# A mixture-of-experts stage whose experts are ranked by row count: big ones as before, small ones in 64-row tiles

## The chip, the cores and the metric

The kernel runs on one core of a Trainium2 chip. The metric is the device time of one execution in microseconds (us); the median of several executions is compared.

## The reference, cut to what matters

A decoder block: two mixers (causal pooling and sparse attention), a residual, and then a mixture of 32 gated-MLP experts with top-2 routing inside one of four groups. Everything is float32. The change touches the experts alone:

```python
for each expert e, with the rows xb of h2 that were routed to it:   # 1024 tokens, 2 experts each
    a  = silu(xb @ w_gate[e]) * (xb @ w_up[e])    # (n_e, 2048) @ (2048, 512), twice
    ys = a @ w_down[e]                            # (n_e, 512) @ (512, 2048)
    out[token] += ys * gate                       # 2048 rows in all, 64 an expert on average
x = x + gt2 * out
return rmsnorm(x, g_final)
```

Each expert's weights are 12 MiB and are read once, 384 MiB in all.

## The kernel before

The routing runs on the chip. `tables` leaves `sidx` (128 x 32, int32: for each expert and slot the token, or a number past the end for an empty slot), `sgat` (the gates, same layout) and `cnt` (rows of each expert, on every partition).

Then the experts run one after the other, 0 to 31. An expert has `CAP` = 112 slots. `gather` fetches its token rows from the scratch tensor `h2_d` by an indirect DMA from GpSimd's queue (L1221); slots past the end move nothing. `columns_of` transposes the 128 x 2048 rows on TensorE in sixteen 128 x 128 pieces (L1232) and splits each group of four into a high part `xh`, rounded to the matmul's fast fp32 type by ScalarE, and a rest `xl`, by VectorE (both L112, in `split`).

Weights come in twelve 1 MiB chunks an expert (`weight_chunks`: four of gate, four of up, four of down), issued by SyncE (`load`, L1246) into thirteen `raw` buffers, about one expert ahead; the buffer order is the order of use. `halves` splits a chunk in two steps into `hi` (ScalarE) and `lo` (VectorE), each 128 x 1024. `mm3` then forms one product as three fast matmuls, hi x hi, lo x hi, hi x lo (L117, L120, L121; 128 x 512 columns each). An expert has 32 such products for gate and up and 16 for down, 144 matmuls.

In `hidden` the next expert's columns are transposed between the up and the down matmuls (`nxt`), so that TensorE has work while sigmoid and the products of `sg` are formed (L1269 to L1271). `expert` ends with the gating of the output: ScalarE multiplies by the gate (L1295), GpSimd by the row `gt2` (L1296). `scatter` adds the rows to `ya_d` by an indirect DMA (L1300). The last expert isn't scattered: a tail adds its rows by a matmul with a one-hot `pick`, adds `ya_d` and normalises the eight token blocks (L1498 to L1527).

Between the first nine weight loads and the first expert stands a loop for overflow (`For_i`): its trip count, read by every engine from `ni`, is the number of extra blocks of rows of experts with more than 112 rows; it is computed by VectorE from `cnt` (L1371 to L1383). A trip would compute one expert with buffers of its own.

The order of instructions on each engine is that of the program, moved by the framework's scheduler except where `last(...)` pins it.

Elsewhere in the kernel unsplit fp32 matmuls already run: L418 multiplies 32-column stationaries by 512 columns of `w_ada`, the outputs cycling over four strips of 32 partitions; L916 uses one strip alone; L1009 forms the router's logits.

Of the kernel before, what the change touches and what calls it, by code (L numbers as in the profile page):

```python
# [19 lines left out]
P = 128  # L20
D = 2048
KT = D // P
S = 1024
# [4 lines left out]
TINY = 1.1754944e-38  # L28
RATE, RATE2 = 27, 19
NH = 8  # L30
CAP = 112
NE = 32
NG = 4
DE = 512
# [40 lines left out]
def hybrid_block(ctx, tc, x, c, w_ada, b_ada, g_mix, w_in, w_pool, pool_scale, rel_bias, w_out,  # L75
# [32 lines left out]
    def tr_ps():  # L108
        return psum.tile([P, 512], F32, name="tr", bufs=4)
# [841 lines left out]
    rk = rt.tile([P, 2, NB], F32, name="rk")  # L951
    cnt = rt.tile([P, NE], F32, name="cnt")
    sidx = rt.tile([P, NE], I32, name="sidx")
    sgat = rt.tile([P, NE], F32, name="sgat")
    gt2r, gfr = [rt.tile([KT, P], F32, name=n) for n in ("gt2r", "gfr")]
    with ExitStack() as es:
# [108 lines left out]
        def tables(hf):  # L1065
# [30 lines left out]
            nc.vector.tensor_add(tb0, tb0, pa[:, :96])  # L1096
            nc.vector.tensor_scalar(dmp, tb0[:, 64:], -1.0, 1.0, op0=OP.mult, op1=OP.add)
            nc.vector.tensor_scalar(dmp, dmp, pid, float(S), op0=OP.mult, op1=OP.add)
            nc.vector.tensor_add(sidx, dmp, tb0[:, :32])
            nc.vector.tensor_copy(sgat, tb0[:, 32:64])  # L1100
            pc = tr_ps()
            for i in range(NB):
# [111 lines left out]
                finish(1, st)  # L1214
    wo1.close()

    def gather(A, idx, fill=False):
        xg = A.xg()
        if fill:
            nc.gpsimd.memset(xg, 0.0)  # L1220
        nc.gpsimd.indirect_dma_start(out=xg[:CAP], out_offset=None, in_=h2_d,  # L1221
                                     in_offset=bass.IndirectOffsetOnAxis(ap=idx[:CAP], axis=0),
                                     bounds_check=S - 1, oob_is_err=False)
        return xg

    def columns_of(A, xg):
        xh, xl = A.xh(), A.xl()
        for k4 in range(4):
            pt = tr_ps()
            for j in range(4):  # L1230
                k = k4 * 4 + j
                nc.tensor.transpose(pt[:, j * P:(j + 1) * P], xg[:, k * P:(k + 1) * P], ident)  # L1232
            ks = slice(k4 * 4, k4 * 4 + 4)
            split(xh[:, ks, :], xl[:, ks, :], pt.rearrange("p (a b) -> p a b", b=P))
        return xh, xl
# [22 lines left out]
    def hidden(A, chunks, xh, xl, nxt=None):  # L1258
        pgu = []
        for _ in range(2):  # L1260
            ps, k = mm_ps(), 0
            for k0 in range(0, KT, 4):
                for w in halves(A, chunks()):
                    mm3(ps, (xh[:, k, :], xl[:, k, :]), w, k == 0, k == KT - 1)
                    k += 1
            pgu.append(ps)
        wd0 = halves(A, chunks())
        sg = A.sg()
        nc.scalar.activation(sg, pgu[0], AF.Sigmoid)  # L1269
# [14 lines left out]
    def expert(A, chunks, gt2, xh, xl, gate, nxt=None):  # L1284
        ah, al, w, res = hidden(A, chunks, xh, xl, nxt)
# [12 lines left out]

    def scatter(y, idx):
        nc.gpsimd.indirect_dma_start(out=ya_d, out_offset=bass.IndirectOffsetOnAxis(ap=idx[:CAP], axis=0),  # L1300
                                     in_=y[:CAP], in_offset=None, compute_op=OP.add,
                                     bounds_check=S - 1, oob_is_err=False)

    class Tiles:
# [7 lines left out]
        def sg(self):  # L1312
            return self.x.tile([P, DE], F32, name="sg")

        def ah(self):
            return self.x.tile([P, 4, P], F32R, name="ah")

        def al(self):
            return self.m.tile([P, 4, P], F32R, name="al")

        def xh(self):
            return self.m.tile([P, KT, P], F32R, name="xh")

        def xl(self):
            return self.m.tile([P, KT, P], F32R, name="xl")
# [34 lines left out]
    srcs = [c_ for e in range(NE) for c_ in weight_chunks(w_gate[e], w_up[e], w_down[e])]  # L1360
    early = deque(load(A, srcs.pop(0)) for _ in range(9))
    xgs = deque(gather(A, sidx[:, e:e + 1], True) for e in range(2))


    NOV = 20
    with ExitStack() as es:
        ov = pool_of(es, "ov")
        slot = ov.tile([P, P], F32, name="slot")
        nc.gpsimd.iota(slot, pattern=[[1, P]], base=0, channel_multiplier=0, allow_small_or_imprecise_dtypes=True)
        nb = ov.tile([P, NE], F32, name="nb")  # L1370
        nc.vector.tensor_scalar(nb, cnt, float(CAP), None, op0=OP.is_gt)  # L1371
        for j in range(2, -(-S // CAP)):
            nc.vector.scalar_tensor_tensor(nb, cnt, float(j * CAP), nb, op0=OP.is_gt, op1=OP.add)
        ce = nb
        d = 1
        while d < NE:
# [12 lines left out]
        ei = ov.tile([P, NE], F32, name="ei")  # L1389
        nc.gpsimd.iota(ei, pattern=[[1, NE]], base=0, channel_multiplier=0, allow_small_or_imprecise_dtypes=True)  # L1390
        nc.gpsimd.iota(od, pattern=[[1, NOV]], base=0, channel_multiplier=0, allow_small_or_imprecise_dtypes=True)
        nov = nc.values_load(ni[0:1, 0:1], min_val=0, max_val=NOV - 1)
        with tc.For_i(0, nov, 1) as it:
            with ExitStack() as e2:
# [9 lines left out]
                nc.vector.tensor_scalar(oj, oj, 1.0, float(CAP), op0=OP.add, op1=OP.mult)  # L1404
                nc.vector.tensor_scalar(oi, oe_, float(NE - 1), None, op0=OP.min)
                ej = lp.tile([P, 2], F32, name="ej")
                nc.vector.tensor_copy(ej[:, 0:1], oe_[:, bass.ds(it, 1)])
                nc.vector.tensor_copy(ej[:, 1:2], oj[:, bass.ds(it, 1)])
                ex_ = nc.values_load(oi[0:1, bass.ds(it, 1)], engines=[mybir.EngineType.SP], min_val=0,
                                     max_val=NE - 1)  # L1410
                oh1 = lp.tile([P, NE], F32, name="oh1")
                nc.vector.tensor_scalar(oh1, ei, ej[:, 0:1], None, op0=OP.is_equal)
                pt_ = tr_ps()
                for t in range(NB):
                    for j in range(2):
# [21 lines left out]
                xh, xl = columns_of(B, gather(B, ix, True))  # L1437
                parts = iter(list(weight_chunks(*[w[bass.ds(ex_, 1)].rearrange("o a b -> (o a) b")
                                                  for w in (w_gate, w_up, w_down)])))
                y, _ = expert(B, lambda: load(B, next(parts)), g2_, xh, xl, od_[:, 1:2])  # L1440
                scatter(y, ix)

    m = pool_of(mo_, "mo")
    A.m, A.halves = m, [(mh, 2), (mh, 2), (m, 2), (m, 2)]
    A.raws += [(m, 4)] * 4
    early.extend(load(A, srcs.pop(0)) for _ in range(4))
    xe = columns_of(A, xgs.popleft())

    def chunks():
        return early.popleft() if early else load(A, srcs.pop(0))  # L1450

    for e in range(NE - 1):
        def nxt(e=e):
            x_ = columns_of(A, xgs.popleft())
            if e + 2 < NE:
                xgs.append(gather(A, sidx[:, e + 2:e + 3]))
            return x_

        y, xe = expert(A, chunks, gt2, *xe, sgat[:, e:e + 1], nxt)
        scatter(y, sidx[:, e:e + 1])  # L1460


    ah, al, w, _ = hidden(A, chunks, *xe)
# [3 lines left out]
    nc.vector.tensor_copy(sid, sidx[:, NE - 1:NE])  # L1467
# [19 lines left out]
    for n4 in range(4):  # L1487
        if n4 % 2 == 0:
            yh, yl = A.hilo()
        gated(y, py[n4], sgat[:, NE - 1:NE], gt2, n4)  # L1490
        ys.append((yh[:, n4 % 2, :], yl[:, n4 % 2, :]))
        split(*ys[n4], y[:, n4 * 512:(n4 + 1) * 512])

# [74 lines left out]
```

## Time and profile before

| | us |
|---|---|
| median of 3 executions | 2880.85 (2875.68 to 2884.74) |
| profiled execution: its own time | 2879.47 |
| profiled execution: span, first to last instruction | 2877.6 |
| mean granted TensorE clock over the span | 0.96 of 2.4 GHz |

The rows further down are of that one profiled execution; their times count from the first instruction. Busy time of an engine is the time in which at least one of its instructions ran. A matmul's record lasts longer than the step from one matmul to the next, since matmuls overlap; the step is read from the starts.

### The profile page before, as it was taken

The numbers are of one execution on the slowest core, as the hardware profiler recorded it, in microseconds if no ns is written. First come the engines' busy times: TensorE is split into PE (matmuls) and PEld (weight loads), VectorE is DVE, ScalarE is ACT, GpSimd is POOL, SyncE is SP. The second block draws the span as 40 slices with busy tenths as digits, with TensorE's granted clock in tenths as the row PEclk, the third lists the DMA queues.
The fourth block names the chain that finished last, engine by engine and source line by source line (L and its number), as shares of the span: only waits on it lengthen the run. The fifth ranks groups of instructions, "written<-read, shape, count | busy, mean of one in ns | idle before, by whom it ended". The sixth has DMA issues, their size and how long they took to land.

```text
span 2877.6 us, 37030 instructions
## 1 busy us (share of the span) xinstructions
PE 2571.0 (89%) x11968; PEld 2041.0 (71%) x11968; DVE 2172.6 (75%) x3098; ACT 1851.6 (64%) x2856; POOL 1129.9 (39%) x943
## 2 busy tenths in 40 slices
PE   6978888999988899999985999999999999999994
PEld 3667677887756677788874777777777777777773
DVE  6798776888853773344437888888888888888988
ACT  6636777888544773243234777777777777777775
POOL 2286877655863310434222333233332233332222
PEclk8989999999999999999997999999999999999996
DMA  8734555666566614544466999999999999999974
GB/s 306 266 121 125 160 157 149 203 208 191 168 197 208 173 38 162 179 156 144 161 227 236 346 349 350 345 344 341 340 346 346 360 352 348 342 356 341 347 263 166
DMA packets 301223, 713.47 MB, mean 248 GB/s; under 512 B 33196, under 2 KB 189956, under 8 KB 243236
## 3 DMA queue, kind: packets, MB, share of 16 engines
q1 hardware_dynamic: 292960, 678.04, 66.4%
q0 software_dynamic: 8064, 33.02, 5.0%
q8 instruction: 96, 1.57, 0.2%
q14 instruction: 103, 0.84, 0.1%
HBM read 655.37 MB, written 80.38 MB: 256 GB/s over the span
## 4 chain that ended last, share of the span: by engine, by line
PE 52%; DVE 16%; ACT 9%; issue 9%; DMA 8%; POOL 4%; SPq 1%; ACTq 0%; DVEq 0%; POOLq 0%
PE mm L117 14%; PE mm L120 14%; PE mm L121 13%; DMA adw<-in_w_ada_dram 5%; DVE lo L112 3%; POOL adacc L526 3%; PE tr L1232 2%; ACT y L1295 2%; ACT adp L521 2%; ACT hi L112 2%; PE tr L120 1%; PE tr L117 1%; PE tr L121 1%; DVE wlo L112 1%; ACT tk_junk L560 1%
## 5 line engine op out<-in xcount | busy, mean ns | idle before, releaser
L112 DVE TENSOR_TENSOR lo<-raw,hi 128x1024 fp32r<-128x1024 f32 x768 | 972.0, 1318 | 130.6 <-ACT hi L112 126.0
L112 ACT CAST hi<-raw 128x1024 fp32r<-128x1024 f32 x768 | 778.7, 1053 | 217.0 <-PE mm L121 210.1
L526 POOL TENSOR_TENSOR adacc<-adacc,adp 128x256 f32<-128x256 f32 x480 | 428.7, 894 | 194.7 <-ACT adp L521 169.2
L120 PE MATMUL mm<-lo,xh 128*128 128x512 f32 x1024 | 412.3, 403 | 43.0 <-DVE lo L112 42.8
L121 PE MATMUL mm<-hi,xl 128*128 128x512 f32 x1024 | 400.1, 391 | 0.0
L117 PE MATMUL mm<-hi,xh 128*128 128x512 f32 x1024 | 398.8, 391 | 0.0
L1296 POOL TENSOR_TENSOR y<-y,gt 128x512 f32<-128x512 f32 x124 | 258.1, 2112 | 189.8 <-ACT y L1295 189.8
L521 ACT ACTIVATE adp<-adw,cs 128x256 f32<-128x256 f32 x480 | 235.9, 505 | 149.8 <-DMA adw<-in_w_ada_dram 73.5
L1221 POOL DMA_INDIRECT xg<-h_d,sidx x32 | 48.9, 1529 | 667.7 <-PE tr L1232 639.1
L120 PEld LDWEIGHTS mm<-lo,xh 128*128 128x128 f32 x1024 | 192.3, 188 | 127.9 <-DVE lo L112 91.5
L117 PEld LDWEIGHTS mm<-hi,xh 128*128 128x128 f32 x1024 | 192.5, 188 | 41.0
L121 PEld LDWEIGHTS mm<-hi,xl 128*128 128x128 f32 x1024 | 192.5, 188 | 36.8 <-DVE xl L112 0.7
L120 PE MATMUL mm<-hTl,whi 128*128 128x512 f32 (+1 forms) x544 | 206.4, 380 | 9.9 <-DVE hTl L476 8.7
L117 PE MATMUL mm<-hTh,whi 128*128 128x512 f32 (+1 forms) x544 | 206.3, 381 | 0.9 <-ACT whi L112 0.9
L121 PE MATMUL mm<-hTh,wlo 128*128 128x512 f32 (+1 forms) x544 | 204.3, 377 | 1.3 <-DVE wlo L112 1.3
L120 PE MATMUL mm<-lo,ah 128*128 128x512 f32 x512 | 201.3, 393 | 0.0
L112 DVE TENSOR_TENSOR olo<-oraw,ohi 128x1024 fp32r<-128x1024 f32 x64 | 93.0, 1455 | 135.9 <-ACT ohi L112 135.8
L121 PE MATMUL mm<-hi,al 128*128 128x512 f32 x512 | 187.9, 398 | 0.0
L688 DVE SCALAR_TENSOR_TENSOR sc<-ev,wi,sc 128x512 f32<-128x512 f32 (+3 forms) x150 | 135.1, 937 | 58.5 <-ACT ev L684 58.3
L121 PE MATMUL mm<-ohi,ml 128*128 128x512 f32 x448 | 175.7, 392 | 0.0
L117 PE MATMUL mm<-ohi,mh 128*128 128x512 f32 x448 | 175.6, 393 | 0.0
L120 PE MATMUL mm<-olo,mh 128*128 128x512 f32 x448 | 175.4, 392 | 0.0
(370 smaller groups left out, 5416.8 us busy)
## 6 DMA issues: line engine op xcount, KB each, us to landing
raw<-in_w_gate_dram SPq DMA_DIRECT2D x128, 1024.0 KB
raw<-in_w_up_dram SPq DMA_DIRECT2D x128, 1024.0 KB
raw<-in_w_down_dram SPq DMA_DIRECT2D x128, 1024.0 KB
adw<-in_w_ada_dram SPq DMA_DIRECT2D x512, 128.0 KB
wt<-in_w_ada_dram SPq DMA_DIRECT2D x64, 512.0 KB
oraw<-in_w_out_dram SPq DMA_DIRECT2D x64, 512.0 KB
wraw<-in_w_in_dram SPq DMA_DIRECT2D x60, 512.0 KB
xt<-in_x_dram SPq DMA_DIRECT2D x8, 1024.0 KB
```

The source lines that it names most:

```text
L112: for i in (nc.scalar.copy(hi, src), nc.vector.tensor_sub(lo, src, hi.bitcast(F32))):
L117: i = nc.tensor.matmul(o, a[0], b[0], start=first, stop=False)
L120: nc.tensor.matmul(o, a[0], b[1], start=False, stop=False)
L121: nc.tensor.matmul(o, a[1], b[0], start=False, stop=final)
L521: last(nc.scalar.mul(dst, adw.pop(i), cs[:, k:k + 1]))
L526: nc.gpsimd.tensor_add(acc[r, n], acc[r, n], adp.pop(i))
L560: nc.scalar.activation(jk, sc[b], AF.Sign, bias=t, scale=1.0, accum_out=cn[:, j:j + 1])
L688: nc.vector.scalar_tensor_tensor(sc[b][:, c0:c0 + w], rl[:, :w], wi[:, b, h:h + 1], sc[b][:, c0:c0 + w], op0=OP.mult, op1=OP.add)
L1221: nc.gpsimd.indirect_dma_start(out=xg[:CAP], out_offset=None, in_=h2_d, in_offset=bass.IndirectOffsetOnAxis(ap=idx[:CAP], axis=0), bounds_ ...
L1232: nc.tensor.transpose(pt[:, j * P:(j + 1) * P], xg[:, k * P:(k + 1) * P], ident)
L1295: nc.scalar.mul(y[:, ns], py[n4], gate)
L1296: nc.gpsimd.tensor_mul(y[:, ns], y[:, ns], gt2[:, ns])
```

## The change

The ranking: a key per expert (32 x rows + 31 - index; expert 0 gets the greatest) is compared with all others, which gives each expert a place. A one-hot matrix `moved` of places permutes the slot tables by matmul into `pidx`, `pgat` and the list `ordi` of expert numbers in order of place. Places 0 to 15 are big (112 slots, computed as before), 16 to 31 small (`CAP2` = 64 slots). They run in the order 0, 16, 17, 1, 18, 2, 19, ..., 14, 31, 15: two small ones at first, then alternating, with a big one last. Expert 0 is always first, and its weights are addressed statically; the others' by a number that SyncE reads from `ordi`.

A small expert transposes 64 rows only and keeps the columns unsplit (`xT`). Its weight chunks are not split either: plain fp32 matmuls read the raw chunk, with 64-column stationaries; even and odd contraction steps go to the two halves of the partitions of one bank, and `folds` (two identities on top of each other) adds the halves and transposes them in one matmul. The down product puts two of its four column ranges in each half. The gating is one VectorE operation for each 512 columns, in big experts too.

The overflow loop counts blocks past 112 or 64 slots.

```diff
-CAP = 112
+CAP, CAP2, NBIG = 112, 64, 16
...
-            nc.vector.tensor_add(sidx, dmp, tb0[:, :32])
+            nc.vector.tensor_add(sidf, dmp, tb0[:, :32])
+            nc.vector.tensor_copy(sidx, sidf)
...
+    def few_columns_in_steps(A, xg, pin=None):
+        xT = A.xT()
+        for k8 in range(2):
+            pt = tr_ps()
+            for j in range(8):
+                k = k8 * 8 + j
+                i = nc.tensor.transpose(pt[:, j * CAP2:(j + 1) * CAP2], xg[:CAP2, k * P:(k + 1) * P],
+                                        ident[:CAP2, :CAP2])
+                if pin and k == 0:
+                    pin(i)
+            nc.scalar.copy(xT[:, k8 * 8:k8 * 8 + 8, :], pt.rearrange("p (a b) -> p a b", b=CAP2))
+            yield xT
...
         for n4 in range(4):
-            ns = slice(n4 * 512, (n4 + 1) * 512)
-            nc.scalar.mul(y[:, ns], py[n4], gate)
-            nc.gpsimd.tensor_mul(y[:, ns], y[:, ns], gt2[:, ns])
+            gated(y, py[n4], gate, gt2, n4)
         return y, res
...
+    def few(A, chunks, gt2, xT, gate, nxt):
+        pf = tr_ps()
+        sums = [A.sg(), A.us()]
+        sig, aT = A.sig(), A.aT()
+
+        def fold(i):
+            for f in range(4):
+                nc.tensor.matmul(pf[:, (i * 4 + f) * CAP2:(i * 4 + f + 1) * CAP2], sums[i][:, f * P:(f + 1) * P], folds,
+                                 start=True, stop=True)
+
+        for i in range(2):
+            ps, k = mm_ps(), 0
+            for k0 in range(0, KT, 4):
+                raw = chunks()
+                for j in range(4):
+                    h = k % 2 * CAP2
+                    nc.tensor.matmul(ps[h:h + CAP2, :], xT[:, k, :], raw[:, j, :], start=(k < 2), stop=(k >= KT - 2))
+                    k += 1
+                if i == 1 and k0 == 4:
+                    fold(0)
+                    nc.scalar.activation(sig, pf[:, :4 * CAP2], AF.Sigmoid)
+                    nc.vector.tensor_mul(sig, sig, pf[:, :4 * CAP2])
+            nc.scalar.copy(sums[i][:, :256], ps[:, :256])
+            nc.vector.tensor_copy(sums[i][:, 256:], ps[:, 256:])
+        steps = nxt()
+        for _, res in zip(range(3), steps):
+            pass
+        fold(1)
+        nc.vector.tensor_mul(aT.rearrange("p a b -> p (a b)"), sig, pf[:, 4 * CAP2:])
+        for res in steps:
+            pass
+        py = [mm_ps() for _ in range(2)]
+        for k in range(4):
+            raw = chunks()
+            for n4 in range(4):
+                h = n4 % 2 * CAP2
+                nc.tensor.matmul(py[n4 // 2][h:h + CAP2, :], aT[:, k, :], raw[:, n4, :], start=(k == 0), stop=(k == 3))
+        y = A.y()
+        for n4 in range(4):
+            h, ns = slice(n4 % 2 * CAP2, n4 % 2 * CAP2 + CAP2), slice(n4 * 512, (n4 + 1) * 512)
+            nc.vector.scalar_tensor_tensor(y[:CAP2, ns], py[n4 // 2][h, :], gate[h], gt2[h, ns], op0=OP.mult, op1=OP.mult)
+        return y, res
...
+        e = nc.values_load(ordi[0:1, r:r + 1], engines=[mybir.EngineType.SP], min_val=0, max_val=NE - 1)
+        return weight_chunks(*[w[bass.ds(e, 1)].rearrange("o a b -> (o a) b") for w in (w_gate, w_up, w_down)])
...
-    xgs = deque(gather(A, sidx[:, e:e + 1], True) for e in range(2))
+    x0 = gather(A, sidx[:, 0:1], fill=True)
...
+        nc.vector.scalar_tensor_tensor(key, cnt, float(NE), kb, op0=OP.mult, op1=OP.add)
+        nc.vector.scalar_tensor_tensor(own, key[:NE], 1.0, ident[:NE, :NE], op0=OP.mult, op1=OP.mult,
+                                       accum_out=place[:, 0:1])
+        nc.vector.tensor_scalar(own, key[:NE], place[:, 0:1], 0.0, op0=OP.is_gt, op1=OP.add, accum_out=place[:, 1:2])
+        nc.vector.tensor_scalar(place[:, 2:3], place[:, 1:2], float(NBIG), None, op0=OP.is_ge)
+        nc.vector.tensor_scalar(flag, ident[:NE, :NE], place[:, 2:3], None, op0=OP.mult)
+        pk = tr_ps()
+        last(nc.tensor.matmul(pk[:, :NE], onesb[:NE, :], flag, start=True, stop=True))
+        nc.vector.tensor_scalar(cap, pk[:, :NE], float(CAP2 - CAP), float(CAP), op0=OP.mult, op1=OP.add)
+        nc.vector.tensor_scalar(moved, ei[:NE], place[:, 1:2], None, op0=OP.is_equal)
+        nc.vector.tensor_sub(over, cnt, cap)
...
-    early.extend(load(A, srcs.pop(0)) for _ in range(4))
-    xe = columns_of(A, xgs.popleft())
+    early.extend(load(A, next(srcs)) for _ in range(3))
+    cols = columns_of(A, x0)
...
+    for i, t in enumerate((sidf, sgat)):
+        nc.tensor.transpose(pt[:NE, i * P:(i + 1) * P], t, ident)
+    nc.scalar.copy(flip, pt[:NE, :2 * P].rearrange("e (a p) -> e a p", p=P))
+    pm = tr_ps()
+    for i in range(2):
+        nc.tensor.matmul(pm[:, i * NE:(i + 1) * NE], flip[:, i, :], moved, start=True, stop=True)
+    nc.tensor.matmul(pm[:NE, 2 * NE:3 * NE], pid[:NE, 0:1].to_broadcast([NE, NE]), moved, start=True, stop=True)
+    nc.vector.tensor_copy(ordi, pm[0:1, 2 * NE:3 * NE])
...
+    for i in range(NE - 1):
+        def nxt(i=i):
+            yield from (columns_in_steps if seq[i + 1] < NBIG else few_columns_in_steps)(A, xgs.popleft(), last)
+            if i + 2 < NE:
+                xgs.append(gather_of(i + 2))
+
+        big, r = seq[i] < NBIG, seq[i]
+        y, cols = (expert if big else few)(A, chunks, gt2, cols, pgat[:, r:r + 1], nxt)
+        scatter(y, pidx[:, r:r + 1], CAP if big else CAP2)
```

`columns_in_steps` is `columns_of` as a generator that yields after each of its four groups. `gather` and `scatter` take the number of slots.

## Rows read from the trace of the kernel before

**Rows 1.** The page: GB/s in 40 equal slices; indirect queue (packets, MB, share).

```profile
GB/s 306 266 121 125 160 157 149 203 208 191 168 197 208 173 38 162 179 156 144 161 227 236 346 349 350 345 344 341 340 346 346 360 352 348 342 356 341 347 263 166
...
q0 software_dynamic: 8064, 33.02, 5.0%
```

**Rows 2.** Windows: length, busy us (instructions) of each engine, clock, DMA share, GB/s.

```profile
core 0: us, PE busy (x) PEld busy (x) DVE busy (x) ACT busy (x) POOL busy (x), PEclk, DMA share, GB/s
2200.00:2300.00 100.00, 92.89 (x423) 73.11 (x423) 88.03 (x83) 74.23 (x86) 25.77 (x13) 1.00 0.98 356
44.00:46.00 2.00, 1.73 (x10) 0.57 (x13) 0.34 (x2) 0.00 (x0) 0.00 (x0) 0.50 0.75 237
1540.00:1549.00 9.00, 0.00 (x0) 0.00 (x0) 0.15 (x1) 0.24 (x1) 0.17 (x2) 0.50 0.32 96
1600.00:2700.00 1100.00, 1019.82 (x4582) 800.55 (x4583) 969.67 (x868) 822.69 (x950) 334.85 (x167) 1.00 0.96 348
1730.00:1740.00 10.00, 8.51 (x43) 6.68 (x42) 9.32 (x12) 7.39 (x10) 0.00 (x0) 1.00 1.01 419
2000.00:2010.00 10.00, 10.00 (x45) 8.01 (x44) 9.43 (x10) 8.39 (x9) 0.00 (x0) 1.00 0.99 331
2776.00:2786.00 10.00, 8.58 (x35) 6.12 (x34) 8.38 (x6) 7.93 (x9) 9.72 (x5) 1.00 0.00 2
2804.00:2810.00 6.00, 6.00 (x28) 4.96 (x27) 5.57 (x6) 4.29 (x5) 0.00 (x0) 1.00 1.02 426
```

**Rows 3.** Waits from 1600 to 2700 us: total us, times, longest us.

```profile
SPq L1246 <- DVE lo L112: 962.0, 335, 6.0
...
ACT hi L112 <- PE mm L121: 181.2, 258, 1.5
...
PEld mm L120 <- DVE lo L112: 82.2, 105, 1.0
...
ACT hi L112 <- DMA raw<-in_w_gate_dram: 2.4, 2, 1.2
```

**Rows 4.** Groups, 1700 to 2700 us: count, busy us, mean ns, idle before, releasers.

```profile
L112 DVE TENSOR_TENSOR lo<-raw,hi 128x1024 fp32r<-128x1024 f32 x610 | 772.7, 1321 | 103.6 <-ACT hi L112 100.9
L112 ACT CAST hi<-raw 128x1024 fp32r<-128x1024 f32 x610 | 617.6, 1053 | 168.1 <-PE mm L121 162.9 <-DMA raw<-in_w_gate_dram 2.4 <-DVE lo L112 0.6
...
L1232 PE MATMUL tr<-ident,xg 128*128 128x128 f32 x408 | 64.7, 276 | 0.3
```

**Rows 5.** Timeline of PE: split matmuls, fp32 in strips, logits.

```profile
2028.01 0.39 PE L117 MATMUL mm<-hi,xh 128*128 128x512 f32 x1
...
2029.82 0.39 PE L121 MATMUL mm<-hi,xl 128*128 128x512 f32 x1
...
44.52 6.66 PE L418 MATMUL tr<-wt,csz 128*32 128x512 f32 x28
...
1499.13 1.08 PE L1009 MATMUL tr<-wr,h2T 128*128 128x36 f32 x8 [0.73 <-ACT h2T L1004]
```

**Rows 6.** Timeline of the end: last weight loads, last casts, gating.

```profile
2757.33 13.63 SPq L1246 DMA_DIRECT2D raw<-in_w_down_dram  x4
...
2807.34 2.01 ACT L112 CAST hi<-raw 128x1024 fp32r<-128x1024 f32 x2 [0.27 <-PE mm L121]
...
2812.39 2.73 DVE L1282 SCALAR_TENSOR_TENSOR y<-mm,sgat,gt 128x512 f32<-128x512 f32 x4 [1.61 <-issue]
```

**Rows 7.** Groups over the whole span: the fp32 matmul in one strip.

```profile
L916 PE MATMUL tr<-ra,ones 128*32 128x512 f32 x32 | 17.4, 626 | 2.4 <-DMA ra<-acc_d 2.4
```

**Rows 8.** Timeline from the row counts to the first expert.

```profile
1536.39 1.77 DVE L1373 SCALAR_TENSOR_TENSOR nb<-cnt,nb 128x32 f32<-128x32 f32 x8
...
1540.04 0.15 DVE L1383 CAST ni<-ce 128x1 int32<-128x1 f32 x1
...
1549.14 1.97 SPq L1246 DMA_DIRECT2D raw<-in_w_down_dram  x3
...
1550.10 3.68 PE L1232 MATMUL tr<-ident,xg 128*128 128x128 f32 x16 [10.48 <-DVE sid L1467]
```

More of the change, by code (lines that the diff above doesn't have):

```diff
@@ L953, in hybrid_block @@
     sidx = rt.tile([P, NE], I32, name="sidx")
+    sidf = rt.tile([P, NE], F32, name="sidf")
     sgat = rt.tile([P, NE], F32, name="sgat")
@@ L1215, in hybrid_block, with gather @@
     wo1.close()
-    def gather(A, idx, fill=False):
+    def gather(A, idx, rows=CAP, fill=False):
         xg = A.xg()
@@ L1220, in gather, with columns_in_steps @@
             nc.gpsimd.memset(xg, 0.0)
[L1221 to L1222 removed]
+        nc.gpsimd.indirect_dma_start(out=xg[:rows], out_offset=None, in_=h2_d,
+                                     in_offset=bass.IndirectOffsetOnAxis(ap=idx[:rows], axis=0),
                                      bounds_check=S - 1, oob_is_err=False)
         return xg
[L1226 removed]
+    def columns_in_steps(A, xg, pin=None):
         xh, xl = A.xh(), A.xl()
@@ L1302, in scatter @@
+    def scatter(y, idx, rows=CAP):
+        nc.gpsimd.indirect_dma_start(out=ya_d, out_offset=bass.IndirectOffsetOnAxis(ap=idx[:rows], axis=0),
+                                     in_=y[:rows], in_offset=None, compute_op=OP.add,
                                      bounds_check=S - 1, oob_is_err=False)
@@ L1359, in hybrid_block, with weights_of @@
     spread(gt2, gt2r)
-    srcs = [c_ for e in range(NE) for c_ in weight_chunks(w_gate[e], w_up[e], w_down[e])]
-    early = deque(load(A, srcs.pop(0)) for _ in range(9))
-    xgs = deque(gather(A, sidx[:, e:e + 1], True) for e in range(2))
-    NOV = 20
+    def weights_of(r):
+        if r == 0:
+            return weight_chunks(w_gate[0], w_up[0], w_down[0])
+        e = nc.values_load(ordi[0:1, r:r + 1], engines=[mybir.EngineType.SP], min_val=0, max_val=NE - 1)
+        return weight_chunks(*[w[bass.ds(e, 1)].rearrange("o a b -> (o a) b") for w in (w_gate, w_up, w_down)])
+    seq = [0, NBIG, NBIG + 1]
+    for r in range(1, NBIG - 1):
+        seq += [r, r + NBIG + 1]
+    seq.append(NBIG - 1)
+    assert sorted(seq) == list(range(NE))
+    srcs = (c_ for r in seq for c_ in weights_of(r))
+    early = deque(load(A, next(srcs)) for _ in range(9))
+    x0 = gather(A, sidx[:, 0:1], fill=True)
+    ordi = mg.tile([1, NE], I32, name="ordi")
+    pidx = mg.tile([P, NE], I32, name="pidx")
+    pgat = mg.tile([P, NE], F32, name="pgat")
+    folds = mg.tile([P, CAP2], F32, name="folds")
+    moved = mg.tile([NE, NE], F32, name="moved")
+    nc.gpsimd.tensor_add(folds, ident[:, :CAP2], ident[:, CAP2:])
+    NOV = 24
     with ExitStack() as es:
@@ L1436, in hybrid_block @@
                 row_bc(g2_, row_d[3])
-                xh, xl = columns_of(B, gather(B, ix, True))
+                cols = columns_of(B, gather(B, ix, fill=True))
                 parts = iter(list(weight_chunks(*[w[bass.ds(ex_, 1)].rearrange("o a b -> (o a) b")
                                                   for w in (w_gate, w_up, w_down)])))
-                y, _ = expert(B, lambda: load(B, next(parts)), g2_, xh, xl, od_[:, 1:2])
+                y, _ = expert(B, lambda: load(B, next(parts)), g2_, cols, od_[:, 1:2])
                 scatter(y, ix)
@@ L1445, in hybrid_block, with gather_of @@
     A.raws += [(m, 4)] * 4
-    early.extend(load(A, srcs.pop(0)) for _ in range(4))
-    xe = columns_of(A, xgs.popleft())
-    def chunks():
[L1450 to L1463, printed above, removed]
+    early.extend(load(A, next(srcs)) for _ in range(3))
+    cols = columns_of(A, x0)
+    flip = A.us()[:NE, :2 * P].rearrange("e (a p) -> e a p", p=P)
+    pt = tr_ps()
+    for i, t in enumerate((sidf, sgat)):
[6 more added lines that the diff above has]
+    nc.vector.tensor_copy(ordi, pm[0:1, 2 * NE:3 * NE])
+    nc.vector.tensor_copy(pidx, pm[:, :NE])
+    nc.vector.tensor_copy(pgat, pm[:, NE:2 * NE])
+    nc.vector.tensor_copy(pgat[CAP2:, NBIG:], pm[:CAP2, NE + NBIG:2 * NE])
+    def chunks():
+        return early.popleft() if early else load(A, next(srcs))
+    def gather_of(i):
+        return gather(A, pidx[:, seq[i]:seq[i] + 1], CAP if seq[i] < NBIG else CAP2, i == 1)
+    xgs = deque([gather_of(1)])
+    for i in range(NE - 1):
[6 more added lines that the diff above has]
+        scatter(y, pidx[:, r:r + 1], CAP if big else CAP2)
+    r_last = seq[-1]
+    ah, al, w, _ = hidden(A, chunks, *cols)
     ids, pick = A.xg()[:, :S], A.xg().bitcast(F32R)[:, :S]
```

56 lines of the change are left out of this document (38 added, 18 removed).

## The prediction

> **What bounds the kernel now.** I read the slices of the page first: from about 1580 us to 2730 us, the experts, the traffic stands at 340 to 360 GB/s where it is 38 to 306 before [rows 1]. So the stage comes close to some limit of the transfers, and the question is whether they set its pace. The windows say that they don't quite: over 1600 to 2700 us DMA is 0.96 busy at 348 GB/s, PE is busy 93%, its granted clock is 1.00 [rows 2]. The waits decide. SyncE, which issues the weight loads, spent 962 of 1100 us waiting for VectorE's lo, that is, for a weight buffer to come free, and the one engine that reads arriving weights, ScalarE's cast, waited for a load only 2.4 us in all [rows 3]. So loads arrive early and are held back by the consumer. The consumer is a ring of three engines: the cast waits for PE, lo for the cast, PE for lo [rows 3, 4]. One expert takes 39.2 us: 408 token transposes at 16 an expert are 25.5 experts in 1000 us [rows 4]. Of these PE is busy 0.93 x 39.2 = 36.3 us: 144 matmuls at 0.226 us (eight steps from 2028.01 to 2029.82 us [rows 5]) are 32.6, the 16 transposes 64.7 / 25.5 = 2.5 [rows 4], the rest is small. VectorE's lo take 24 x 1.32 = 31.7 and the casts 24 x 1.05 = 25.3 us an expert.
>
> How early the loads are shows at the end: the last four weight loads are issued from 2757 us on, DMA moves only 2 GB/s from 2776 us, and the last weight chunk is cast from 2807.3 us [rows 2, 6]. So about 31 us of lead, most of an expert.
>
> **The change, part by part.**
>
> *Small experts on PE.* A small expert drops 144 matmuls, 24 casts, 24 lo, and gains 48 unsplit fp32 matmuls of 512 columns whose outputs alternate between the two halves of the partitions. The nearest row is L418: 28 records, 14 fp32 matmuls over four column tiles, take 6.66 us at a clock of 0.50, that is 1.2 GHz [rows 2, 5]: 0.476 us each. (An fp32 matmul leaves two records: L916 runs 16 times and leaves 32 [rows 7].) Half as many tiles cost twice that, the full clock (2.4 GHz) halves it again: 0.476 us, and 48 are 22.8 us. If tiles didn't overlap at all, one would cost 4 x 0.476 / 2 = 0.95 us, and 48 would be 45.7 us. L916, one tile alone, agrees with this end: busy 17.4 us for 16, 1.09 us each [rows 7]. I take 22.8, because L418 alternates tiles as the new code does. To it come eight folds at the price of the logits matmuls, 8 records in 1.08 us, 0.27 each [rows 5], 2.2 us; the transposes of the next expert, 2.5 us; and two short waits around the folds, which other transposes partly cover, say 1.5 us: 29 us. Bounds: 27 with no waits, 52 with no overlap.
>
> The Trainium skill (TensorEngine Tiling (Array Packing), Key Properties) says that tiles run in parallel, but that a change of tiling mode drains the engine; against the change, then, there are some six changes of mode in a small expert. A matmul's latency beyond its issue step is 0.39 - 0.226 = 0.16 us [rows 5], so an estimate by that rule is 1 us an expert, inside the bounds above.
>
> *The big experts* keep their matmuls. The gating moves from ScalarE and GpSimd to four VectorE operations, 2.73 us together in the last expert of before [rows 6]; the next expert is mostly a small one without lo, so nothing urgent stands behind them, and its transposes need no split, which saves four VectorE operations. I keep 39.2 us; bounds 36.3 (PE alone) and 42 (the gating uncovered).
>
> *The pair.* Compute: 39.2 + 29 = 68 us where it was 78.4. So the ring stops being the limit, and the weights, whose bytes don't change, become it.
>
> *What DMA needs for an expert.* Twelve loads of 1 MiB are 12.58 MB; gathers and scatters moved 33.02 MB in 63 transfers [rows 1], two of them 1.05 MB. Those bytes don't change: 33.02 MB is 4028 rows of 8 KB, the real rows, not the 112 slots. Fastest: weights alone ran at 419 and 426 GB/s [rows 2], 30.0 us, and the indirect queue took 5.0% of 16 engines' span [rows 1]: 0.05 x 2877.6 x 2 / 63 = 4.6 us; 34.6 together. Slowest: the share as it stands, 0.96 x 39.2 = 37.6, or 38.3 by the fullest 100 us, 0.98 busy at 356 GB/s [rows 2]. Near which? At 2000 to 2010 us the engines are 0.99 busy and move only 331 GB/s [rows 2]: indirect packets also slow the weights beside them, which speaks for the upper end; shares of 1.01 and 1.02 [rows 2] count some packets twice, which speaks for a little less. I take 37.2 us (366 GB/s); with 13 buffers and a consumer 6 us a pair faster DMA has always something to load.
>
> *The start.* The ranking adds about ten VectorE operations of 0.2 us (eight of that size took 1.77 us [rows 8]) and a matmul ahead of the count that the overflow loop reads. Every engine stands still from that count (1540.0 us) until 1549.1 us, although the loop runs no trip [rows 2, 8], so nothing hides it: +2.5 us, all engines resume at 1551.6. The first expert's transposes take 3.7 us [rows 8]; the table of ranks follows on PE (two transposes, three matmuls), with a ScalarE copy and four VectorE copies, some 3.5 us; then SyncE reads the second expert's number and can load it: first bytes at about 1562 us (1558 if the table is built ahead of the transposes, 1568 if the register read is as slow as the loop's). The three static loads after the loop keep DMA busy for about 7 us of that gap. Reads of later numbers cost SyncE little; it has most of its time free [rows 3].
>
> *The sum.* 31 experts are loaded from 1562 us. During the first one buffers come free at its own pace, 39 us; then 30 x 37.2 = 1116: the last weights land at 2717. The lead is used up, so the last chunk is cast as it lands, and from that cast to the end before took 2877.6 - 2807.3 = 70.3 us [rows 6], unchanged work: output adds, norms and writes. The span is 2787. Around the span lie 2879.5 - 2877.6 = 1.9 us, and the profiled execution lies 1.4 us below the median: 2790 us, 3.1% faster.
>
> **The rivals.**
>
> *The transfers gain little rate.* For: 0.96 busy is nearly full, and weights may slow one another when more loads are outstanding. Against: 419 and 426 GB/s without indirect packets. At 356 GB/s an expert needs 38.3 us and the time is 1562 + 39 + 30 x 38.3 + 70.3 + 3.3 = 2824; at 348 it needs 13.63 / 348 = 39.2 as now, only the lead is gained, and the time is 2851.
>
> The Trainium skill has a rule of that kind (DMA: Bandwidth & Descriptors, Where 436 GB/s comes from): the HBM side of a core binds at about 358 GB/s, which is an estimated 38.1 us an expert and 2818 us. The windows of 419 and 426 GB/s [rows 2] disagree with it as a hard limit.
>
> *The two tiles don't overlap* (slower). A small expert takes 52 us, compute rules, and the time is 2881 + 16 x (52 - 39.2) = 3086. For: no row shows 64-column tiles, and in program order the two records of one matmul share a tile. Against: L418. Compute decides from a small expert above 2 x 37.2 - 39.2 = 35.2 us; the kernel is slower from about 39.2.
>
> *The clock falls.* PE is now in short waits, some 1.3 us a chunk in small experts. At 1.2 GHz 48 matmuls are 45.7 us. For: the clock was 0.50 while PE stood still for 9 us [rows 2]. Against: the waits are far shorter, and PE at half rate would no longer wait. With half of each small expert at the low clock it takes 40 us, a pair 79: about 2890.
>
> *A small expert overflows* its 64 slots, so that a loop trip computes a whole expert unhidden: over 70 us. The reference's routing of its default inputs gives 44 to 103 rows an expert; after expert 0 and the fifteen fullest the fullest has 61. No trip.
>
> **Chances.** Bound by DMA at 34.6 to 37.6 us an expert: 0.60 (2712 to 2802, likeliest 2790). Little rate gained, 37.6 to 39.2 us: 0.24 (to 2851). No overlap: 0.08. Clock: 0.06. Overflow: 0.02. About 0.3% (9 us) is what a measurement here can tell from no change. Faster: 0.60 + 0.24 + a third of the clock case, 0.86; same 0.04 and slower 0.10 share the rest. The range 2740 to 2855 leaves out the fastest DMA (0.04) and nearly all of the last three cases (0.14).
>
> **What would show it.** Right: the share of DMA near 1.00 at about 366 GB/s; a pair every 74 us; SyncE no longer waiting for lo, while PE and the cast wait for weight loads; column-tile matmuls starting in pairs, 48 in 21 to 23 us; last load landing within a few us of its cast, then 70 us. Wrong: PE full in small experts with matmuls 0.85 us or more apart; the clock at 0.50 in the stage; DMA still below 350 GB/s while compute waits for it; a second register read or a late rank table keeping DMA idle at each expert's first chunk.

## The result, and the profile after

The changed kernel takes 2787.5 us (median of 4, 2783.9 to 2791.6) where the kernel before, run beside it, takes 2881.7: a ratio of 0.968, 95% interval 0.966 to 0.970. 2790 us was forecast. The profiled execution took 2783.9 us, with a span of 2782.1.

The page's slices after, and its indirect queue:

```profile
GB/s 305 268 143 106 164 161 152 169 229 194 167 171 160 284 73 52 226 156 156 178 136 223 223 379 376 376 381 378 380 372 370 375 378 373 369 366 369 371 394 157
q0 software_dynamic: 6528, 33.07, 5.0%
```

Through the experts the traffic now stands at 366 to 381 GB/s, where it stood at 340 to 360 [rows 1]. The indirect queue moves the same 33 MB in fewer packets. The windows (columns as in [rows 2]):

```profile
1600.00:2600.00 1000.00, 869.93 (x3990) 534.45 (x3986) 526.62 (x573) 387.87 (x466) 66.91 (x54) 0.95 1.00 374
1558.00:1566.00 8.00, 8.00 (x38) 6.37 (x37) 5.69 (x10) 5.26 (x5) 1.92 (x2) 1.00 0.10 23
2319.50:2325.50 6.00, 5.54 (x13) 3.97 (x14) 5.75 (x5) 3.80 (x4) 0.01 (x1) 0.50 1.03 341
2326.00:2340.00 14.00, 14.00 (x64) 11.56 (x63) 11.79 (x11) 10.95 (x12) 0.00 (x0) 1.00 1.00 399
```

DMA is busy for 1.00 of the stage (0.96 before), PE for 87% (93%), VectorE for 53%. The waits of the same 1000 us (SyncE's own and the rest):

```profile
SPq L1267 <- DMA raw<-in_w_gate_dram: 321.4, 108, 5.8
SPq L1267 <- DMA raw<-in_w_up_dram: 270.5, 108, 6.3
SPq L1267 <- DMA raw<-in_w_down_dram: 228.8, 109, 5.6
SPq L1267 <- DVE lo L112: 4.8, 18, 0.4
...
ACT hi L112 <- DMA raw<-in_w_gate_dram: 175.6, 43, 12.3
...
PE mm L1335 <- DMA raw<-in_w_up_dram: 34.1, 28, 3.0
ACT hi L112 <- PE mm L121: 33.0, 61, 3.0
```

This is the mirror of [rows 3]. SyncE waited 962 of 1100 us for lo to free a buffer; now, of 1000 us, 4.8 for lo and 321 + 271 + 229 = 821 for weight loads to land. (The trace shows why SyncE waits for loads at all: they report on eight semaphores in turn, and each goes out right after the eighth load before it has landed.) The cast waited 2.4 us for loads and 181 for PE; now 176 for the gate loads alone and 33 for PE. The page's chain that ended last has DMA for 34% of the span and PE for 7%.

The groups of the stage, and the timeline of PE, first at the start of a large expert, then in a small one:

```profile
L112 DVE TENSOR_TENSOR lo<-raw,hi 128x1024 fp32r<-128x1024 f32 x312 | 364.8, 1221 | 77.2 <-ACT hi L112 73.0
L112 ACT CAST hi<-raw 128x1024 fp32r<-128x1024 f32 x312 | 313.7, 1049 | 228.7 <-DMA raw<-in_w_gate_dram 175.6 <-PE mm L121 33.0 <-DMA raw<-in_w_up_dram 11.7
```

```profile
2319.36 0.80 PE L117 MATMUL mm<-hi,xh 128*128 128x512 f32 x1 [3.78 <-ACT hi L112]
...
2358.09 0.39 PE L121 MATMUL mm<-hi,al 128*128 128x512 f32 x1
2358.41 7.09 PE L1335 MATMUL mm<-raw,xT 128*64 128x512 f32 x32
2365.97 0.66 PE L1326 MATMUL tr<-folds,sg 128*128 128x64 f32 x4 [0.47 <-ACT sg L1341]
...
2372.59 1.94 PE L1335 MATMUL mm<-raw,xT 128*64 128x512 f32 x8 [1.64 <-DMA raw<-in_w_up_dram]
```

In the small expert 32 records are 16 products in 7.09 us, 0.443 each (0.476 was taken); then PE waits for an up load. One more number: lo takes 1221 ns where it took 1321 [rows 4]. The prediction had no reason for that; it became the main finding.

The start and the end of the stage, from the timelines:

```profile
1545.52 0.15 DVE L1500 CAST ni<-ce 128x1 int32<-128x1 f32 x1
1563.22 0.17 DVE L1576 CAST ordi<-tr 1x32 int32<-1x32 f32 x1
```

```profile
1551.76 3.67 PE L1235 MATMUL tr<-ident,xg 128*128 128x128 f32 x16 [10.21 <-ACT hi L112]
...
1562.01 0.63 PE L1574 MATMUL tr<-moved,us 32*128 32x32 f32 x4
```

```profile
1548.68 1.30 SPq L1267 DMA_DIRECT2D raw<-in_w_down_dram  x3
1564.18 2.00 SPq L1267 DMA_DIRECT2D raw<-in_w_gate_dram  x4
...
2678.71 7.80 SPq L1267 DMA_DIRECT2D raw<-in_w_down_dram  x4
```

```profile
2678.67 1.99 ACT L112 CAST hi<-raw 128x1024 fp32r<-128x1024 f32 x2 [6.75 <-DMA raw<-in_w_gate_dram]
...
2707.84 0.58 ACT L112 CAST ah<-tr 128x512 fp32r<-128x512 f32 x1 [3.09 <-PE tr L1296]
...
2713.39 2.01 ACT L112 CAST hi<-raw 128x1024 fp32r<-128x1024 f32 x2 [0.27 <-PE mm L121]
```

The count of the overflow loop is ready 5.5 us later than before [rows 8], and the first load by rank goes out at 1564.2 us. From 1558 to 1566 us DMA was 0.10 busy (the window above). The last load goes out by 2686.5 us, and the last of its 16 parts reports its landing at 2709.1, by the semaphores in the trace. The last expert's first cast waits 6.75 us for its gate load, until 2678.7; the last chunk is cast at 2713.4, and what holds that cast is PE, not a load.

### The profile page after: what moved, and what is told of

The parts are those of the page before. It is cut to its first block, busy times and chain, and to the rows that moved or that the text cites. A ratio compares the mean times of both kernels' runs of the same rounds, so it can differ in the third digit from the quotient of the medians.

```text
span 2782.1 us, 35200 instructions
## 1 busy us (share of the span) xinstructions
PE 2420.8 (87%) x11401; PEld 1762.2 (63%) x11401; DVE 1704.9 (61%) x2805; ACT 1382.7 (50%) x2333; POOL 836.2 (30%) x822
## 5 line engine op out<-in xcount | busy, mean ns | idle before, releaser
L112 ACT CAST hi<-raw 128x1024 fp32r<-128x1024 f32 x384 | 386.7, 1050 | 267.0 <-DMA raw<-in_w_gate_dram 198.3
L112 DVE TENSOR_TENSOR lo<-raw,hi 128x1024 fp32r<-128x1024 f32 x384 | 449.4, 1221 | 96.0 <-ACT hi L112 90.8
L1335 PE MATMUL mm<-raw,xT 128*64 128x512 f32 x1024 | 242.2, 611 | 35.3 <-DMA raw<-in_w_up_dram 34.1
L117 PE MATMUL mm<-hi,xh 128*128 128x512 f32 x512 | 215.4, 421 | 59.7 <-ACT hi L112 59.7
L120 PE MATMUL mm<-lo,xh 128*128 128x512 f32 x512 | 217.0, 424 | 12.3 <-DVE lo L112 12.2
L121 PE MATMUL mm<-hi,xl 128*128 128x512 f32 x512 | 211.6, 413 | 0.0
L1335 PEld LDWEIGHTS mm<-raw,xT 128*64 128x64 f32 x1024 | 68.7, 139 | 175.6 <-issue 116.7
L117 PEld LDWEIGHTS mm<-hi,xh 128*128 128x128 f32 x512 | 104.6, 204 | 95.6 <-ACT hi L112 72.0
L120 PEld LDWEIGHTS mm<-lo,xh 128*128 128x128 f32 x512 | 104.1, 203 | 46.7 <-DVE lo L112 24.7
L121 PE MATMUL tr<-hTh,wlo 128*128 128x512 f32 x320 | 128.6, 404 | 5.4 <-DVE wlo L112 5.4
```

The lines of the kernel that those rows point to most:

```text
L112: for i in (nc.scalar.copy(hi, src), nc.vector.tensor_sub(lo, src, hi.bitcast(F32))):
L117: i = nc.tensor.matmul(o, a[0], b[0], start=first, stop=False)
L120: nc.tensor.matmul(o, a[0], b[1], start=False, stop=False)
L121: nc.tensor.matmul(o, a[1], b[0], start=False, stop=final)
L1335: nc.tensor.matmul(ps[h:h + CAP2, :], xT[:, k, :], raw[:, j, :], start=(k < 2), stop=(k >= KT - 2))
```

## The experiments

Each ran beside the kernel before; ratios are to it, and so is the 0.968 of the changed kernel.

**Do the two tiles run at the same time?** In a small expert, for gate and up (the folds then read 64 rows, and the down products go to four banks instead of two):

```
- h = k % 2 * CAP2
- nc.tensor.matmul(ps[h:h + CAP2, :], xT[:, k, :], raw[:, j, :], start=(k < 2), stop=(k >= KT - 2))
+ nc.tensor.matmul(ps[:CAP2, :], xT[:, k, :], raw[:, j, :], start=(k == 0), stop=(k == KT - 1))
...
```

> The changed kernel with each of a small expert's 48 products put into the same 64 output columns (gate and up in one tile each, down in four banks, folds over 64 rows), so that two products never stand beside each other on TensorE. Theory (the two tiles run at the same time, which brings a 512-column product to 0.443 us each): alone a product takes twice that, a small expert's products 42.5 us instead of 21.3, its whole 48 to 51 us, a pair of experts 87 to 91 us instead of the 72.8 that the loads take, over 15 pairs 210 to 280 us more: 3000 to 3070 us. Rival (a product that fills half of the columns is as quick alone, and the tiles bring nothing): 2780 to 2795 us.

2933.5 us, ratio 1.019 (1.016 to 1.021): the expectation's rival is out, and without the tiles the change would be a loss. From PE's timeline and the windows:

```profile
1806.10 22.53 PE L1334 MATMUL mm<-raw,xT 128*64 128x512 f32 x52
```

```profile
1600.00:2600.00 1000.00, 986.81 (x3511) 534.48 (x3510) 468.26 (x504) 345.41 (x408) 59.23 (x49) 1.00 0.92 336
```

A product alone takes 22.53 / 26 = 0.867 us, 1.96 times the 0.443 in alternating tiles. PE is 99% busy here and DMA 0.92, so this kernel shows what the engines need when loads don't hold them: from the last gating instruction of one expert to that of the next, the trace has 45.6 us for a small expert and 36.2 for a large one. The expectation of 3000 to 3070 was too high on both (51 and 39.2): (45.6 + 36.2 - 72.8) x 15.5 = 140 us more than the changed kernel, 2927, comes within 7 us.

**Do loads set the pace, after and before?** The last chunk is left out in small experts, and in the kernel before in every second expert:

```
- raw = chunks()
+ raw = raw if k in (3,) else chunks()
... [and the list of loads is shortened to match]
```

> The changed kernel, but each of the 16 small experts leaves out the load of its last weight chunk (1 MB) and multiplies with the chunk before it once more: 16 of 384 loads go, no instruction of TensorE does. Theory (after the change the loads set the pace, 36.39 us for an expert's 12, 3.03 each): 16 x 3.03 = 48 us less, 2735 to 2750 us. Rival (the engines still set it; TensorE is 87% busy): nothing to 5 us less, 2780 to 2790 us.

> The kernel before, with the last weight load of every second expert left out (15 of 384) and the chunk before it multiplied once more; all casts and products stay. Theory (before the change the engines set the pace, 39.2 us an expert, and the loads ran 31 us ahead): no change, 2876 to 2885 us. Rival (the loads set it there too, at a share of 0.96): 15 x 3.2 = 48 us less, 2825 to 2840 us.

After: 2747.6 us, ratio 0.954 (0.952 to 0.957), 40 us less than the changed kernel, 2.5 for each load left out. Before: 2876.8 us, ratio 0.999 (0.998 to 1.000), next to nothing. So the bound has moved from the engines to the loads. But a load is worth 2.5 us, not 3.03. The third kernel leaves out three down chunks in a small expert instead of one:

> The changed kernel, but each small expert loads 9 weight chunks instead of 12 and multiplies all of its down products with the one down chunk that it loads. No instruction of TensorE goes. A pair of experts then needs 21 x 3.03 = 63.6 us of loads. Theory (the engines need 37.2 us for a large expert and the 29 us of the prediction for a small one, 66.2 a pair, so they become the bound): (72.8 - 66.2) x 15.5 = 102 us less, some 2685 us. Rival 1 (a small expert needs 26 us or less, the loads stay the bound): 141 us less, some 2647 us. Rival 2 (the engines set the pace already with one load left out, at 2747 us): 2735 to 2750 us.

2668.3 us, ratio 0.926 (0.924 to 0.928): 119 us less for 48 loads, again 2.48 each, between the two forecasts. (By the ratios to the kernel before, the two slopes are 2.4 and 2.5.) The straight line says that loads still set the pace with a quarter of a small expert's loads gone; DMA is 0.99 busy:

```profile
1600.00:2600.00 1000.00, 937.34 (x4472) 585.15 (x4469) 602.69 (x651) 445.78 (x528) 81.03 (x59) 0.99 0.99 370
```

Both forecasts went by 36.4 / 12 = 3.03 us, which spreads the row traffic over the weights. At 2.49 us for 1.05 MB weights move at 421 GB/s, close to the window of 419 with next to no indirect packets [rows 2]. Twelve are 29.9 us. The other 6.5 of an expert's 36.4 us are what is left over; gathers and scatters are the only other traffic of that size, so I put it down to them.

**Does the alternating order matter?**

```
- seq = [0, NBIG, NBIG + 1]
- for r in range(1, NBIG - 1):
-     seq += [r, r + NBIG + 1]
- seq.append(NBIG - 1)
+ seq = list(range(NBIG - 1)) + list(range(NBIG, NE)) + [NBIG - 1]
```

> The changed kernel with another order only: the 15 largest ranks one after the other, then the 16 small ones, then the last large one, instead of alternating. Theory (a large expert needs 39.2 us of the engines and 36.4 of the loads, a small one less of the engines; only alternation lets the loads of a large one be hidden over two experts): the 14 large ones in a row cost 2.8 us each more, 39 us in all, and the small ones give nothing back, since they wait for loads: 2815 to 2835 us. Rival (the buffers ahead level it out, or the order doesn't matter because the loads set the pace everywhere): 2780 to 2795 us.

2788.0 us, ratio 0.968 (0.966 to 0.970): the order is worth nothing, and my theory fell. Two windows, large experts and small ones:

```profile
1650.00:2050.00 400.00, 384.14 (x1747) 307.59 (x1746) 369.07 (x374) 291.70 (x320) 47.78 (x21) 1.00 0.99 364
2200.00:2600.00 400.00, 317.63 (x1452) 111.56 (x1454) 52.39 (x90) 24.97 (x57) 24.71 (x21) 0.93 1.01 384
```

Large experts in a row take 37.2 to 38.6 us, not 39.2, with PE 96% busy and DMA 0.99: engines and loads are nearly level. Small ones take 35.3 on average with PE at 79%. Row traffic would explain why the sum stays: at 6.5 us for the mean of 64 rows, and with 76 rows in a large and 53 in a small expert (counted from the reference's routing), loads need 29.9 + 7.7 = 37.6 and 29.9 + 5.4 = 35.3 us. That split by rows fits the two stretches; it wasn't tried by itself. In alternation a large expert takes 42.6 us and a small one 30.7 on average, 73.2 a pair, which is what the loads give, not what either needs.

**Why a large expert no longer takes 39.2 us.** The gating alone, put into the kernel before:

```
- ns = slice(n4 * 512, (n4 + 1) * 512)
- nc.scalar.mul(y[:, ns], py[n4], gate)
- nc.gpsimd.tensor_mul(y[:, ns], y[:, ns], gt2[:, ns])
+ gated(y, py[n4], gate, gt2, n4)      # one VectorE instruction
```

> The kernel before with one part of the change alone: every expert's result is gated by one VectorE instruction for each 512 columns instead of one on ScalarE and one on GpSimd. Theory of the prediction (moving the gating is worth nothing by itself, a large expert stays at 39.2 us): 2873 to 2885 us. Rival, from the large experts of the run with another order, which took 37.2 to 37.5 us each and whose VectorE residues took 1219 ns instead of 1321 with GpSimd out of the way: 1.0 to 2.0 us off each of 31 experts, 2820 to 2850 us.

2841.7 us, ratio 0.987 (0.985 to 0.988). A part that I had priced at nothing is worth 40 us alone. Which half of the old gating cost it?

Without GpSimd's multiplication, in the kernel before:

> The kernel before, with GpSimd's four multiplications of each expert's result left out (the second of the two factors is missing from the output of 31 experts); ScalarE's four scalings stay. It tells which half of the old gating cost the 40 us that the VectorE gating saved. Theory (GpSimd's multiplications lengthen VectorE's residues from 1222 to 1321 ns, and so the ring of an expert): the larger part of 40 us comes back, 2835 to 2855 us. Rival (ScalarE's four scalings, 691 ns each, hold up the casts): no change, 2873 to 2885 us.

2827.3 us, 51 less and a little more than expected, with all of ScalarE's scalings in place: it was GpSimd. Groups of these two kernels, gating alone first:

```profile
L112 DVE TENSOR_TENSOR lo<-raw,hi 128x1024 fp32r<-128x1024 f32 x631 | 734.3, 1222 | 58.7 <-ACT hi L112 55.3 <-DMA raw<-in_w_gate_dram 0.2
```

```profile
L112 DVE TENSOR_TENSOR lo<-raw,hi 128x1024 fp32r<-128x1024 f32 x637 | 745.1, 1222 | 115.9 <-ACT hi L112 107.9 <-DMA raw<-in_w_down_dram 2.4 <-DMA raw<-in_w_gate_dram 0.2
```

The trace of before shows the cause within one expert. Two windows of its groups, 1986 to 1994.6 us with GpSimd's four multiplications, and 2001 to 2011 us without:

```profile
L112 DVE TENSOR_TENSOR lo<-raw,hi 128x1024 fp32r<-128x1024 f32 x5 | 8.5, 1736 | 1.8 <-ACT hi L112 1.6
L1296 POOL TENSOR_TENSOR y<-y,gt 128x512 f32<-128x512 f32 x4 | 8.4, 2138 | 3.0 <-ACT y L1295 3.0
...
L112 DVE TENSOR_TENSOR lo<-raw,hi 128x1024 fp32r<-128x1024 f32 x8 | 9.2, 1219 | 0.3 <-ACT hi L112 0.3
```

Beside a multiplication a lo takes 1736 ns, otherwise 1219. From 1600 to 2700 us 138 of 671 lo overlap a multiplication, at 1.71 us on average, and the others take 1.22: 4.9 an expert, 4.9 x 0.49 = 2.4 us on an engine of the ring. A mean over the stage, 1321, had hidden that. The Trainium skill (SBUF — State Buffer, SBUF: two separate sides) states the rule: a VectorE instruction with two inputs in SBUF and a GpSimd one that reads SBUF share one pair of ports, which one of them holds for a whole instruction. The rows agree in kind: each of the two gets slower beside the other.

Does that gain count in the changed kernel? Its large experts got the old gating back:

```
- gated(y, py[n4], gate, gt2, n4)
+ ns = slice(n4 * 512, (n4 + 1) * 512)
+ nc.scalar.mul(y[:, ns], py[n4], gate)
+ nc.gpsimd.tensor_mul(y[:, ns], y[:, ns], gt2[:, ns])
```

> The changed kernel with the old gating for the large experts (ScalarE, then GpSimd, for each 512 columns). Theory (with the ranking the loads set the pace, and a large expert of 39.4 us beside a small one of 29 fits into the 72.8 us of a pair's loads): nothing lost, 2783 to 2795 us. Rival (the gating's 1.2 us an expert count here as they did alone, 15 times and more): 2803 to 2815 us.

2789.7 us, ratio 0.969 (0.967 to 0.970): no. Beside small experts no lo was slowed either:

```profile
L1317 POOL TENSOR_TENSOR y<-y,gt 128x512 f32<-128x512 f32 x54 | 67.0, 1272 | 138.5 <-ACT y L1316 138.5
L112 DVE TENSOR_TENSOR lo<-raw,hi 128x1024 fp32r<-128x1024 f32 x312 | 364.3, 1222 | 74.8 <-ACT hi L112 70.5
```

The multiplication now falls into a small expert, which has no lo. So the two parts of the change are two ways to the same limit, and their gains don't add. How near that limit was shows in SyncE's waits from 1600 to 2600 us, with the gating alone and then without the multiplication:

```profile
SPq L1246 <- DVE lo L112: 594.1, 258, 6.0
```

```profile
SPq L1246 <- DVE lo L112: 257.7, 124, 6.0
```

The rest of its waits, 285 and 621 us, are for loads to land: without the multiplication the kernel before already stands mostly at the loads.

**What holds the loads?** Engines waited for loads whose 128 packets, counted off in order, seemed done 4 to 13 us earlier. The semaphores show why: from the first to the last of a load's 16 completions it is 18.4 us on average (loads issued from 1600 to 2600 us), where it was 4.3 before, and the next load of that semaphore goes out only after the last. The index list was dealt out anew:

```
- nc.scalar.copy(flip, pt[:NE, :2 * P].rearrange("e (a p) -> e a p", p=P))
...
+ for b, rows in enumerate((CAP, CAP2)):      # row r goes to slot (r % 16) * rows / 16 + r // 16
...
+     for i in range(2):
+         nc.scalar.copy(fl[:, b, i, :rows].rearrange("e (c a) -> e c a", c=16),
+                        pv[:, i, :rows].rearrange("e (a c) -> e c a", c=16))
...
```

> The changed kernel with the slots of each expert but the first dealt out in another order: the valid rows no longer fill the low slots of the gather's and the scatter's index list but every seventh (large) or fourth (small) one in turn. The rows moved are the same. Theory (neighbouring slots go to the same of the 16 DMA engines, so that the engines of the low slots do all the row traffic and lag behind; one load's 16 parts landed up to 17 us apart, where 4 us was usual before the change): with the parts landing together an expert's loads take 34.7 to 35.8 us instead of 36.4, 2740 to 2770 us, if the engines follow. Rival (the lag has nothing to do with slots): 2782 to 2793 us.

2761.6 us, ratio 0.959 (0.957 to 0.961), 26 us less for the same rows and bytes:

```profile
1600.00:2600.00 1000.00, 887.43 (x4075) 545.44 (x4072) 540.58 (x587) 397.59 (x476) 70.32 (x57) 0.96 1.01 385
```

385 GB/s instead of 374. The control reverses the slots, so that the valid rows stand side by side at the other end:

> A control for the run with dealt slots: the changed kernel with the slots of each expert but the first in reverse order, so that the valid rows lie side by side again, in the high slots instead of the low ones. Same rows, same extra copies as with dealt slots. Theory (what dealing out saves is the uneven share of the DMA engines): as uneven as in the changed kernel, 2782 to 2793 us. Rival (any new order, or the invalid slots coming first, saves it too): 2755 to 2768 us.

2794.4 us, ratio 0.971 (0.969 to 0.972): nothing gained. So it counts that the valid rows are dealt out over the list, not that their order changes; against this control, which has the same extra copies, dealing saves 33 us. That neighbouring slots share a DMA engine is the reading that fits; the records don't name a packet's engine, so it is inferred. And the parts of a load still land 16 us apart with dealt slots. The lag is 15 to 19 us in every kernel in which SyncE waits much for loads, dealt out or not, and 2 us in the one-tile kernel; so it doesn't measure how uneven the rows lie, and what sets it stays open.

**The start.** The tables ahead of the first expert's transposes:

```
+ [the block that builds flip, pm, ordi, pidx, pgat, moved up to here]
  early.extend(load(A, next(srcs)) for _ in range(3))
- cols = columns_of(A, x0)
+ cols = list(columns_in_steps(A, x0, last))[-1]
```

> The changed kernel with the reordered tables (three small products and their copies) put ahead of the first expert's transposes and casts in the program, so that the first load by rank goes out earlier than 1564.2 us. Theory (the loads set the pace and all later ones wait behind that one; DMA was nearly idle from 1558 to 1566 us): 5 to 10 us less, 2776 to 2783 us. Rival (the first expert's own work, delayed by the tables, or the last large expert takes it back): 2784 to 2792 us.

2782.2 us, ratio 0.966 (0.964 to 0.968). From SyncE's timeline:

```profile
1553.83 1.30 SPq L1267 DMA_DIRECT2D raw<-in_w_down_dram  x3
1560.20 1.49 SPq L1267 DMA_DIRECT2D raw<-in_w_gate_dram  x3
```

The first load by rank goes out 4.0 us earlier, the three static ones 5.2 us later. Five us less fits the theory, but the intervals overlap, and in the profiled executions the last load lands at 2708.8 us, no earlier to speak of than 2709.1. Not shown.

**All together**, with the small experts' slots dealt out from the other end:

> The changed kernel with the tables first and the slots dealt out as in the run with dealt slots, and the small experts' slots dealt out from the other end, so that the slots that get one row more are others than in the large experts. If the two gains add up, 26 + 5 us less than the changed kernel: 2750 to 2760 us. If the row traffic was still uneven, some 10 us less than that: 2738 to 2750 us. If both gave the same time back, 2760 to 2768 us.

2751.6 us (median of 5), ratio 0.956 (0.954 to 0.957): 10 us less than with dealt slots alone. The first load by rank goes out at 1557.5 us here and at 1568.2 there, which is as much; so the sum of the two gains came as forecast, though with a third edit in it, and nothing beyond it is seen. It beats both kernels: 4.4% faster than before, where the change alone gave 3.2%.

## Why the prediction was right, and where it wasn't

*The bound before, and the bound after*: right, and shown. Leaving loads out changed nothing before and 2.5 us a load after.

*What DMA needs for an expert*: 37.2 us taken; 13.63 MB at the measured 374 GB/s are 36.4, and by the landings it is 36.6. Inside it the weights stood right (30.0 taken, 29.9 measured), though not for the reason given: the window of 426 GB/s lies after the last weight load has landed (2776.7 us) and holds reads of `ya_d`. The row traffic at its share of busy time, 4.6 us, was the lower bound and is 6.5 by what the left-out loads leave over; the "upper end" was the right side to lean to, with a step of 0.6 to 0.8 us too many.

*The small experts*: 29 us taken. The 48 products come to 48 x 0.443 = 21.3 us (22.8). The one-tile kernel's 45.6 us hold 48 x 0.867 = 41.6 of products, so all the rest is 4.0, not 6.2: an estimate of some 25 us when loads don't hold it. One of the six changes of tiling mode, priced at 0.16 us each, shows as 0.1: the first tile product starts 0.32 us after the last split matmul (2358.09 to 2358.41 us), where the usual step is 0.226. The price of a product came from a row whose clock wasn't 0.50 throughout (0.62 from 48 to 51.2 us); it came out near all the same (0.476 against 0.443).

*The big experts*: this step failed. "I keep 39.2 us" priced the gating's move at nothing, because I looked for what stands behind the four new VectorE operations and not for what the old ones did to their neighbours. It is 36.2 to 37.3 us. By luck the error cost nothing, since loads ruled: a pair needs 36.2 + 25 = 61 us of the engines, not 68, beside 72.8 of loads. Had the loads been quicker, the forecast would have been too slow; had the change been the gating alone, it would have missed 40 us.

*The start*: resumption at 1551.6 us was right (PE's transposes start at 1551.8), though the count came 5.5 us later instead of 2.5; the first bytes came at 1565 us instead of 1562, since split matmuls were put ahead of the tables on PE.

*The sum*: 2787 for the span, 2782.1 measured, and terms compensate. The last weights land at 2709.1 us instead of 2717. The first loaded expert landed at 1611.8 us instead of 1601 (it began 3 us late and took 47 us, not 39), and the 30 after it took 36.6 us each instead of 37.2, 19 us less together. "The last chunk is cast as it lands" was out by 4 us: PE paces the last expert's casts from the fifth on, to 2713.4. From there to the end are 68.7 us (70.3). 2787 - 7.9 + 4.3 - 1.6 = 2782.

*The rivals*. Little rate gained: no, 374 GB/s where it asked for 348 to 356. The rule beside it, the Trainium skill's 358 GB/s (DMA: Bandwidth & Descriptors, Where 436 GB/s comes from), is passed here for 1000 us on end, and by 385 with dealt slots. No overlap: no, and 3086 was too dear; the kernel that enforces it takes 2933. That is still 1.9% slower than before, so the rival's sign was right. The clock: it does fall, after PE stood still for 3.8 us at a large expert's start (window 2319.5 to 2325.5 us: 0.50, that is 1.2 GHz), and is back at 1.00 by 2326; over the stage it is 0.95. Loads set the pace meanwhile, and the price of nearly 100 us that the prediction put on it did not come. Overflow: every engine goes on into the first expert right after the count, as before.

## What to carry to other kernels

Ask of every instruction that a change removes what it did to the engines beside it, and split a mean duration by what runs next to it: 1736 and 1219 ns were both in the 1321. When two resources are nearly level, gains that move the bound don't add up, so try each part alone and in company before crediting it. Price a transfer by leaving some out: the slope (2.5 us a load) and the average (3.0) are different numbers, and the gap between them is the traffic to look at next, here the order of an index list, worth 26 us.

## What the runs showed of the hardware

- A VectorE subtraction with two SBUF inputs (128 x 1024, fp32) takes 1.71 us on average beside a GpSimd multiplication and 1.22 otherwise; the multiplication (128 x 512) takes 2.11 us beside such subtractions (kernel before) and 1.27 without them (changed kernel with the old gating).
- Two 64-column tiles run their fp32 products side by side almost perfectly: 0.443 us a product of 512 columns in alternation, 0.867 in one tile, at a granted clock of 1.00.
- Gathers and scatters of the same rows cost 26 to 33 us less in 31 experts when the valid indices are dealt out evenly over the list than when they stand side by side, at either end.
- 1 MiB weight loads cost about 2.5 us each at the margin, beside indirect traffic, and 3.0 on average with it.
- From the first to the last of the 16 parts of a 1 MiB load it is 18.4 us on average in the changed kernel, where loads set the pace, and 4.3 in the kernel before.
